# Group A's keys transposed in pairs of heads, and the second layer's units in another order

## The chip, the cores and the metric

The kernel runs on one core of a Trainium2 chip. The metric is the device time of one execution in microseconds. Three runs of the kernel before took 485.81, 486.31 and 487.1 us; the median is 486.31.

## The reference

Two layers, each with a residual connection around one mixer. A layer normalises its 512 x 1024 input, multiplies it by one combined matrix of 3488 columns, cuts the result into parts for four head groups A to D, multiplies each group's output by a SiLU gate, and sends all 1024 columns through an output matrix. The change touches group A, attention over four heads with low-rank queries and keys:

```python
    q = (rmsnorm(cq, mla_q_norm_g) @ mla_w_uq).reshape(B, S, MLA_HEADS, MLA_QK)
    kv = (rmsnorm(ckv, mla_kv_norm_g) @ mla_w_ukv).reshape(B, S, MLA_HEADS, MLA_NOPE + MLA_V)
...
    k = jnp.concatenate([k_nope, jnp.broadcast_to(k_rope, (B, S, MLA_HEADS, MLA_ROPE))], axis=-1)
    o_a = causal_attention_blocks(q, k, v_a, MLA_QK ** -0.5).reshape(B, S, GROUP_WIDTH)
```

A key has 96 numbers: 64 of its own head (`k_nope`, normalised) and 32 rotary ones (`k_rope`), which all four heads share. Queries have 96 too. All is in float32.

## The kernel before

**Tiling.** Tokens lie in four tiles of 128 (NT = 4). Every float32 product is made of three TensorE products of a high and a low part (`mm3`, line 283): an operand is split into `hi`, a copy rounded to the matmul's format, and `lo`, what is left of it, by one operation of ScalarE or VectorE and one of VectorE (`split2`, `split_scaled`).

**Order.** The program is unrolled Python. A small planner (`Order`, `Chain`, `Slots`, lines 75 to 214) runs generators against a clock of its own, prices each operation by a formula (lines 181 to 200; line 188 for VectorE, `cost` at line 217 for a matmul), and issues it on its engine when its inputs are due by that clock. So it fixes each engine's order of instructions; the hardware runs each engine's queue in that order and waits on semaphores. Main work (`main`) issues the large products, one unit of 24 matmuls after another; the heads' work is put between them when it is due, with a higher priority. A `Slots` object counts the buffers of a kind: a generator that asks for a buffer when none is free stops until one is put back, and other generators go on. The tag `t2` has NT2 = 11 buffers of 128 x 512 and serves nearly all temporaries: operands of the heads, gates, sums.

**Units.** In the second layer the order of units is SEQ1 (line 48). The names ga, gb, gc, gd are the gates of the four groups, su, ch, cc, cb inputs of groups B and C, each in two halves of 128 columns; p11, p21, p3, p4, p2, p1, p22 are the seven products from which the token-wise parts (sq: group C's second input and group D's queries; kv: group D's keys and values) are made. Then come seven more products of the output matrix (ZPROD, line 50): b11, t3, b21, t4, t2, t1, b22. b11 takes y tiles 2, 0, 1, 3 in this order (K0 and KK in line 49); y tiles 0 and 1 come from group A, 2 and 3 from group B (gated by gb0 and gb1), 4 and 5 from C, 6 and 7 from D. The first layer has another order (SEQ, line 382).

**Weights.** Units are loaded by SP's queue into `raw` buffers (`load_units`, line 407), split into `whi` and `wlo` by ScalarE and VectorE (`split_units`, `low_half`), and freed. Some weights are sums of others that DMAs add up in DRAM (`t_sums`, line 358, on SP's and POOL's queues).

**Group A.** `low_stats` (line 967) makes the rotary part of the keys, `krt`, 128 x 4 tiles x 32, turns it by six operations of VectorE (`rope`, line 916), and copies it with one POOL operation into columns 64 to 96 of all four heads of `L.K` (line 993); then event `kr_ev` is set. `q_chain` and `kv_chain` fill `L.Q` and the first 64 columns of `L.K`. `mla_heads` (line 1511) waits for all of these, in the second layer also for p4 (`mla_go`). For each head `prep` starts two generators `part` (line 1522): four transposes of 128 tokens x 96 into a PSUM bank (`t0` for queries, `t1` for keys), then the split into two `t2` buffers; keys are scaled by a column of gains, `pcol[0:96, 6 + l]`. When both are there, `qk` issues the scores (tile `sa`), four blocks with three matmuls each; `free` puts four `t2` buffers back, and the next head's `prep` begins.

**Mixer of group C.** `mix_chain` (line 1123) loads `sgw` when event `sg_go` comes (after the unit SGLOAD), masks it on POOL after `mix_go` (after p2), splits it, waits for the four normalised token tiles `vn`, lets MIXLAG pass on the planner's clock, and issues the products `mp`.

**Gains.** `load_rows` (line 615) loads rows of gains with DMAs from POOL's queue into a tile of ones; one transpose turns them into `pcol`.

Of the kernel before, what the change touches and what calls it, by code (L numbers as in the profile page):

```python
# [11 lines left out]
F32 = mybir.dt.float32  # L12
# [20 lines left out]
WSLACK = 300.0  # L33
AHEAD, URGENT, VSLACK = 4, 2, 300.0
NWARM, FILL, FILLEND = 6, 0.9, 15000.0
MIXT, MIXLAG, ROWT, COLT = 44000.0, 2000.0, 36000.0, 17500.0
KSPLIT, HMEAN = 6, 0.0
PAIRS = {}
LOPRIO = -5
# [5 lines left out]
STOK = (1,)  # L45
SPROD = ("p11", "p21", "p3", "p4", "p2", "p1", "p22")
SSUMS = {"p3": 0, "p2": 1, "p1": 2, "p22": 0}
SEQ1 = ['p11', 'ga0', 'p21', 'p3', 'p4', 'ga1', 'p2', 'ch0', 'p1', 'p22', 'cc0', 'gd0', 'gd1', 'su0', 'cb0', 'gb0', 'ch1', 'gc0', 'cc1', 'cb1', 'gb1', 'su1', 'gc1']
K0, K1, KK = (2, 3, 0, 1), (4, 5, 6, 7), (0, 2, 3, 1)
ZPROD = ("b11", "t3", "b21", "t4", "t2", "t1", "b22")  # L50
TS0 = 62000.0
SGLOAD = 'p4'
TAIL = ((0, 256), (256, 512))

C_CQ, C_KV, C_GA, C_CH, C_CB, C_CC, C_GB = 0, 256, 416, 672, 928, 1184, 1440
# [166 lines left out]
def hybrid_trunk(ctx: ExitStack, tc: tile.TileContext, x, positions, norm_g, w_c, w_f, w_t, w_o, mla_q_norm_g,  # L222
# [117 lines left out]

    tsum = {(l, n): dr.tile([2, P, 1024], F32, name=f"{n}_{l}") for l in SEVEN for n in ("t1", "t2", "t3", "t4")}
    tsum_ev = {(l, n, j): Event() for l, n in tsum for j in range(2)}
    ysc = {l: dr.tile([KT, P, S], F32, name=f"ysc_{l}") for l in SEVEN}

    def quad(l, n, j):
# [269 lines left out]
    def load_rows():  # L615
        pr = prow[0]
        nc.gpsimd.dma_start(pr[0:4, 0:P], dram(mla_q_norm_g, 0, [[P, 4], [1, P]]))
        nc.gpsimd.dma_start(pr[4:6, 0:P], dram(mla_kv_norm_g, 0, [[P, 2], [1, P]]))
        nc.gpsimd.dma_start(pr[6:8, 0:64], dram(mla_q_g, 0, [[96, 2], [1, 64]]))
        nc.gpsimd.dma_start(pr[10:12, 0:64], dram(mla_k_nope_g, 0, [[64, 2], [1, 64]]))  # L620
        for i, g in ((8, moba_q_g), (12, moba_k_g)):
            nc.gpsimd.dma_start(pr[i:i + 2, 0:P].rearrange("r (h d) -> r h d", h=2)[:, :, 16:64],
                              dram(g, 16, [[64, 2], [0, 2], [1, 48]]))
# [343 lines left out]
    def low_stats(L, t, a, t0, done):  # L967

        ch = Chain(o, t0)
        ssq, krt = L.ssq, L.krt  # L970
        for i, (c0, c1) in enumerate(((384, 416), (256, 384), (0, 256))):
            yield from ch.act(A.activation, junk[:, :c1 - c0], a[:, c0:c1], AF.Square, scale=(c1 - c0) ** -0.5,
                              accum_out=ssq[:, t, 2 - i:3 - i])
        m = sm.tile([P, 8], F32, tag="ms", name=f"ms{t}_{L.l}")
        e1, e2 = EPS, EPS * EPS
        if L.l == 0:
            yield from ch.wait(v_ev)
            e1, e2 = rv(RE, t), rv(REE, t)
        yield from ch.dve(V.tensor_scalar, m[:, 0:2], ssq[:, t, 1:3], 1.0, e1, op0=ALU.mult, op1=ALU.add)
        yield from ch.dve(V.tensor_scalar, L.e2[:, t, :], ssq[:, t, 0:2], EPS, e2, op0=ALU.mult, op1=ALU.add)  # L980
        yield from pow_rstd(ch, m[:, 4:6], m[:, 0:2], 2)
        L.ms[t] = m
        o.set(L.stat[t], ch.t)
        yield from ch.dve(V.scalar_tensor_tensor, krt[:, t, :], in0=a[:, 384:416], scalar=m[:, 5:6], in1=L.gr,
                          op0=ALU.mult, op1=ALU.mult)
        done(ch)
        L.kr_left -= 1
        if L.kr_left:
            return
        yield from ch.wait(rope_ev)  # L990
        yield from rope(ch, krt, 16, cosT, sinT, f"k{L.l}")
        yield from ch.wait(L.QK_ev)
        yield from ch.pool(G.tensor_copy, L.K[:, :, :, 64:96], krt.unsqueeze(2).to_broadcast([P, NT, 4, 32]))
        o.set(L.kr_ev, ch.t)

    def low_chain(L, t, a, t0, slots):
# [35 lines left out]
    def q_chain(L, t, q_ps, t0):  # L1032
        ch = Chain(o, t0)
        l = L.l
        if not L.QK_taken:
            L.QK_taken = True
            L.Q = yield from tkS.get(ch, f"Q{l}", 96)
            L.K = yield from tkS.get(ch, f"K{l}", 96)
            o.set(L.QK_ev, ch.t)
        yield from ch.wait(L.QK_ev)  # L1040
        Q = L.Q
# [469 lines left out]
    def mla_heads(L):  # L1511
# [3 lines left out]
        if L.stok:  # L1515
            yield from ch0.wait(L.mla_go)

        def prep(H):
            H.prep_ev = [Event(), Event()]
            H.op = [None, None]  # L1520

            def part(i, src):
                ch = Chain(o)
                tp = yield from trS.get(ch, f"t{i}{H.name}")
                for t in range(NT):
                    yield from ch.pe(109.0, PE.transpose, tp[:96, t * P:(t + 1) * P], src[:, t, H.h, :], ident)
                if H.h == 3:
                    tkS.put(ch)
                hi = yield from t2S.get(ch, f"hi{i}{H.name}", F32R)
                lo = yield from t2S.get(ch, f"lo{i}{H.name}", F32R)  # L1530
                if i == 0:
                    yield from split2(ch, hi[:96], lo[:96], tp[:96])
                else:
                    yield from split_scaled(ch, hi[:96], lo[:96], tp[:96], pcol[0:96, 6 + L.l:7 + L.l])
                trS.put(ch)
                H.op[i] = (hi, lo)
                o.set(H.prep_ev[i], ch.t)

            def free(ch):
                for _ in range(4):  # L1540
                    t2S.put(ch)
            H.free = free
            o.spawn(part(0, L.Q))
            o.spawn(part(1, L.K))
            return
            yield

        def qk(ch, H, qt, s):
            (qh, ql), (kh, kl) = H.op
            n = (qt + 1) * P  # L1550
            yield from mm3(ch, n, s, qh[:96, qt * P:n], ql[:96, qt * P:n], kh[:96, :n], kl[:96, :n], True, True)

# [573 lines left out]
```

## Time and profile before

| | |
|---|---|
| runs | 485.81, 486.31, 487.1 us; median 486.31 |
| span of the profiled execution, first to last instruction | 485.2 us |
| instructions of TensorE: matmuls, weight loads | 2432, 2432 |
| VectorE, ScalarE, POOL instructions | 898, 906, 189 |
| DMA packets, bytes | 40223, 92.89 MB, mean 191 GB/s |

The profile gives the span of its execution, and no separate time for it; the runs' median lies 1.1 us above the span.

The page of the profile gives each engine's busy time, then the span in 40 slices, then the chain of work that ended last, then groups of like instructions. A matmul's duration is a latency: the next one starts before it ends, so the time that an instruction takes from TensorE is the distance between starts, read in the order of time. In the tile view, the three numbers are the shortest, the median and the longest duration in ns, then come the first and the last start in us. A row of the waits reads: who waited, for whom, microseconds in total, times, the longest. In the view by stretches each engine's busy time is followed by its count of instructions, and the last three columns are the granted clock, the DMA engines' busy share and GB/s.

### The profile page before, as it was taken

How to read it: one execution, taken by the hardware profiler on the slowest of the kernel's cores; microseconds unless marked ns; L12 is line 12 of the kernel's file. 1: busy time of each engine (PE TensorE's matmuls, PEld its weight loads, DVE VectorE, ACT ScalarE, POOL GpSimd, SP SyncE). 2: the span in 40 equal slices, each digit the busy share in tenths (PEclk: the TensorE clock that was granted, in tenths of full speed). 3: DMA queues.
4: the chain of work that ended last, by engine and by line, in shares of the span. 5: the costliest groups of instructions: out<-in, count | busy, mean ns of one | idle time of the engine just before them, and what ended most of it. 6: DMA issues, size and time to landing. Idle time of an engine off the chain costs nothing.

```text
span 485.2 us, 7553 instructions
## 1 busy us (share of the span) xinstructions
PE 479.2 (99%) x2432; PEld 408.3 (84%) x2432; DVE 402.4 (83%) x898; ACT 330.7 (68%) x906; POOL 118.2 (24%) x189
## 2 busy tenths in 40 slices
PE   8999999999999999999999999999999999999996
PEld 7988888888888888888899888888888888888875
DVE  3598887877988898679998688797897889997992
ACT  6897857776466765457577799678766788576550
POOL 8857711610330014100031014630021300000000
PEclk9999999999999999999999999999999999999999
DMA  7923053998798499885673286696832826436862
GB/s 257 313 85 111 1 217 130 235 264 175 263 227 206 172 240 264 302 281 177 211 241 131 87 273 210 178 279 168 207 97 89 192 93 193 152 109 235 296 206 89
DMA packets 40223, 92.89 MB, mean 191 GB/s; under 512 B 5606, under 2 KB 21304, under 8 KB 39800
## 3 DMA queue, kind: packets, MB, share of 16 engines
q1 hardware_dynamic: 26864, 79.43, 46.9%
q0 software_dynamic: 13216, 12.91, 17.4%
q8 instruction: 19, 0.31, 0.3%
q14 instruction: 20, 0.16, 0.1%
q10 hardware_dynamic: 104, 0.07, 0.1%
HBM read 84.53 MB, written 33.03 MB: 242 GB/s over the span
## 4 chain that ended last, share of the span: by engine, by line
PE 90%; DVE 4%; DMA 3%; SPq 1%; issue 1%; ACT 0%; DVEq 0%
PE cq L209 6%; PE kv L209 6%; PE oy L209 5%; PE cb L209 5%; PE gb L209 5%; PE gc L209 5%; PE cc L209 5%; PE gd L209 5%; PE su L209 5%; PE ch L209 5%; PE ga L209 5%; PE sq L209 5%; PE py L209 3%; PE sa L209 3%; PE pz L209 2%; PE px L209 2%
## 5 line engine op out<-in xcount | busy, mean ns | idle before, releaser
L374 POOL DMA_DIRECT2D t<-in_w_o_dram x16 | 17.9, 1298 | 43.6 <-DMA t<-t 43.2
L179 ACT ACTIVATE pa<-pa,mna 128x384 f32<-128x384 f32 (+3 forms) x50 | 26.4, 554 | 2.1 <-DVE mna L179 2.1
L179 ACT ACTIVATE phd<-pTd 128x512 fp32r<-128x512 f32 (+3 forms) x32 | 13.9, 436 | 18.0 <-PE pTd L209 17.9
L179 DVE CUSTOM_DVE_ANT_0 pa<-sa,maskb,rs_q 128x512 f32<-128x512 f32 (+3 forms) x32 | 16.6, 548 | 10.2 <-PE sa L209 5.2
L179 ACT ACTIVATE whi_t<-raw_t 128x512 fp32r<-128x512 f32 x32 | 18.9, 620 | 5.5 <-DMA raw_t<-t 5.4
L179 ACT ACTIVATE pd<-pd,mnd 128x384 f32<-128x384 f32 (+3 forms) x38 | 20.7, 554 | 2.6 <-DVE mnd L179 2.1
L179 ACT ACTIVATE pha<-pTa 128x512 fp32r<-128x512 f32 (+3 forms) x32 | 13.9, 434 | 12.1 <-PE pTa L209 11.6
L209 PE MATMUL cq<-whi_c,hTh 128*128 128x416 f32 x64 | 20.7, 368 | 0.7 <-ACT hTh L179 0.7
L179 DVE TENSOR_TENSOR wlo_t<-raw_t,whi_t 128x512 fp32r<-128x512 f32 x32 | 20.6, 682 | 0.0
L209 PE MATMUL cq<-wlo_c,hTh 128*128 128x416 f32 x64 | 20.0, 358 | 0.0
L179 DVE TENSOR_TENSOR wlo_p<-raw_p,whi_p 128x512 fp32r<-128x512 f32 x28 | 19.0, 698 | 1.1 <-ACT whi_p L179 0.9
L209 PE MATMUL cq<-whi_c,hTl 128*128 128x416 f32 x64 | 19.8, 356 | 0.0
L179 ACT ACTIVATE whi_b<-raw_b 128x512 fp32r<-128x512 f32 x24 | 14.4, 623 | 7.6 <-DMA raw_b<-in_w_o_dram 7.6
L179 DVE TENSOR_TENSOR pla<-pTa,pha 128x512 fp32r<-128x512 f32 (+3 forms) x32 | 15.1, 486 | 5.1 <-ACT pha L179 5.0
L179 DVE CUSTOM_DVE_ANT_0 pd<-sd,maskb,rs_mq 128x512 f32<-128x512 f32 (+3 forms) x32 | 17.0, 545 | 2.6 <-PE pTd L209 2.3
L374 POOL DMA_DIRECT2D p<-in_w_t_dram x8 | 10.9, 1645 | 29.5 <-DMA p<-p 19.6
L179 DVE TENSOR_TENSOR pld<-pTd,phd 128x512 fp32r<-128x512 f32 (+3 forms) x32 | 15.5, 485 | 2.8 <-ACT phd L179 2.6
L179 DVE TENSOR_TENSOR wlo_b<-raw_b,whi_b 128x512 fp32r<-128x512 f32 x24 | 15.7, 683 | 0.1
L179 ACT ACTIVATE whi_p<-raw_p 128x512 fp32r<-128x512 f32 x25 | 15.0, 624 | 1.0 <-DMA raw_p<-in_w_t_dram 0.6
L179 POOL TENSOR_TENSOR rs_mk<-rs_mk,nhalf 128x16 f32<-128x16 f32 x2 | 6.1, 3074 | 33.8 <-DVE rs_mk L179 33.8
L209 PE MATMUL pTa<-ident,pa 128*128 128x128 f32 x80 | 14.1, 273 | 0.0
L179 POOL TENSOR_SCALAR xss<-xss 128x1 f32<-128x1 f32 x4 | 2.7, 669 | 46.6 <-ACT jk L179 42.3
(488 smaller groups left out, 1868.7 us busy)
## 6 DMA issues: line engine op xcount, KB each, us to landing
t<-in_w_o_dram POOLq DMA_DIRECT2D x16, 512.0 KB, 7.6
raw_t<-t SPq DMA_DIRECT2D x16, 512.0 KB, 5.0
raw_b<-in_w_o_dram SPq DMA_DIRECT2D x12, 512.0 KB, 4.4
t<-in_w_o_dram SPq DMA_DIRECT2D x8, 512.0 KB, 5.4
p<-in_w_t_dram POOLq DMA_DIRECT2D x8, 512.0 KB, 13.7
t<-t SPq DMA_DIRECT2D x8, 512.0 KB, 5.4
raw_p<-p SPq DMA_DIRECT2D x8, 512.0 KB, 4.4
ys<-ysc SPq DMA_DIRECT2D x14, 256.0 KB, 5.7
```

The source lines that it names most:

```text
L179: f(*a, **k)
L209: f(*a, **k)
L374: nc.gpsimd.dma_start(src(l, n, j), src(l, y, j), accum_op=ALU.add, max_dma_last_dim=1024)
```

## The change

The nope parts of the keys of two heads, 2 x 64 columns, are transposed together: four transposes of 128 x 128 a pair, whose upper 64 rows are one head and whose lower 64 rows the other. Each head's half is split into rows 0 to 64 of two `t2` buffers. The rotary part is transposed once a layer, all four tiles in one instruction of 128 x 128 (`krT`), scaled and split by one ScalarE and one VectorE operation, stored to DRAM (`krd`) by eight DMAs of SP, and loaded into rows 64 to 96 of each head's two key buffers by two DMAs of SP a head. A pair takes its four key buffers at its first head. `kr_ev` is set 3 us later on the planner's clock than the stores are issued. `L.K` gets 64 columns a head and no POOL copy. The gains' rows for `pcol` hold each gain twice, for both halves. In the second layer ga1, gd1, gc0, gb0 and others change places, `sgw` is loaded after p2 instead of p4, and MIXLAG is 1000 instead of 2000.

```diff
-MIXT, MIXLAG, ROWT, COLT = 44000.0, 2000.0, 36000.0, 17500.0
+MIXT, MIXLAG, ROWT, COLT = 44000.0, 1000.0, 36000.0, 17500.0
...
-SEQ1 = ['p11', 'ga0', 'p21', 'p3', 'p4', 'ga1', 'p2', 'ch0', 'p1', 'p22', 'cc0', 'gd0', 'gd1', 'su0', 'cb0', 'gb0', 'ch1', 'gc0', 'cc1', 'cb1', 'gb1', 'su1', 'gc1']
+SEQ1 = ['p11', 'ga0', 'p21', 'p3', 'p4', 'p2', 'ch0', 'p1', 'p22', 'cc0', 'gd0', 'ga1', 'su0', 'gc0', 'ch1', 'cc1', 'gd1', 'cb0', 'cb1', 'gb1', 'su1', 'gb0', 'gc1']
...
-SGLOAD = 'p4'
+SGLOAD = 'p2'
...
+    krd = {l: dr.tile([2, 32, S], F32, name=f"krd_{l}") for l in range(DEPTH)}
...
-        nc.gpsimd.dma_start(pr[6:8, 0:64], dram(mla_q_g, 0, [[96, 2], [1, 64]]))
-        nc.gpsimd.dma_start(pr[10:12, 0:64], dram(mla_k_nope_g, 0, [[64, 2], [1, 64]]))
+        for i, g, w in ((6, mla_q_g, 96), (10, mla_k_nope_g, 64)):
+            nc.gpsimd.dma_start(pr[i:i + 2, 0:P].rearrange("r (h d) -> r h d", h=2), dram(g, 0, [[w, 2], [0, 2], [1, 64]]))
...
-        yield from ch.wait(L.QK_ev)
-        yield from ch.pool(G.tensor_copy, L.K[:, :, :, 64:96], krt.unsqueeze(2).to_broadcast([P, NT, 4, 32]))
+        tp = yield from trS.get(ch, f"krT{L.l}")
+        yield from ch.pe(109.0, PE.transpose, tp[:, 0:P], krt.rearrange("p t d -> p (t d)"), ident)
+        z = yield from t2S.get(ch, f"kr{L.l}", F32R)
+        f = -(96 ** -0.5)
+        yield from ch.act(A.activation, z[:, 0:P], tp[:, 0:P], AF.Copy, scale=f)
+        yield from ch.dve(V.scalar_tensor_tensor, z[:, P:2 * P], in0=tp[:, 0:P], scalar=f, in1=z[:, 0:P].bitcast(F32),
+                          op0=ALU.mult, op1=ALU.subtract)
+        trS.put(ch)
+        for i in range(2):
+            for t in range(NT):
+                nc.sync.dma_start(krd[L.l][i, :, t * P:(t + 1) * P], z[t * 32:(t + 1) * 32, i * P:(i + 1) * P].bitcast(F32))
+        ch.t += 3000.0
+        t2S.put(ch)
         o.set(L.kr_ev, ch.t)
...
-            L.K = yield from tkS.get(ch, f"K{l}", 96)
+            L.K = (yield from tkS.get(ch, f"K{l}", 96)).rearrange("p a b c -> p (a b c)")[:, 0:D]
+            L.K = L.K.rearrange("p (t h d) -> p t h d", t=NT, h=4)
...
+            def keys():
+                ch = Chain(o)
+                c2, w = Chain(o), {}
+                for y in range(2):
+                    for i in range(2):
+                        w[y, i] = yield from t2S.get(c2, f"k{i}{y}{H.name}", F32R)
+                        dma(c2, P * 512, w[y, i][64:96, :].bitcast(F32), krd[L.l][i])
+                    o.set(pair["dma", y], c2.t)
+                tp = yield from trS.get(ch, f"t1{H.name}")
+                for t in range(NT):
+                    yield from ch.pe(109.0, PE.transpose, tp[:, t * P:(t + 1) * P],
+                                     L.K[:, t, 2 * hp:2 * hp + 2, :].rearrange("p h d -> p (h d)"), ident)
+                if hp == 1:
+                    tkS.put(ch)
+                for y in range(2):
+                    a0 = y * 64
+                    yield from split_scaled(ch, w[y, 0][0:64], w[y, 1][0:64], tp[a0:a0 + 64],
+                                            pcol[a0:a0 + 64, 6 + L.l:7 + L.l])
+                    pair[y] = w[y, 0], w[y, 1]
+                    o.set(pair["ev", y], max(ch.t, pair["dma", y].t))
+                trS.put(ch)
...
-            o.spawn(part(0, L.Q))
-            o.spawn(part(1, L.K))
+            if x == 0:
+                for y in range(2):
+                    pair["ev", y], pair["dma", y] = Event(), Event()
+                o.spawn(keys())
+            o.spawn(queries())
+            H.prep_ev[1] = pair["ev", x]
...
-            (qh, ql), (kh, kl) = H.op
+            (qh, ql), (kh, kl) = H.op[0], pair[H.h % 2]
```

`queries` is the old `part` for the queries alone.

More of the change, by code (lines that the diff above doesn't have):

```diff
@@ L1516, in mla_heads @@
             yield from ch0.wait(L.mla_go)
+        pair = {}
         def prep(H):
@@ L1520, in prep, with queries @@
             H.op = [None, None]
-            def part(i, src):
+            hp, x = H.h // 2, H.h % 2
+            def queries():
                 ch = Chain(o)
-                tp = yield from trS.get(ch, f"t{i}{H.name}")
+                tp = yield from trS.get(ch, f"t0{H.name}")
                 for t in range(NT):
-                    yield from ch.pe(109.0, PE.transpose, tp[:96, t * P:(t + 1) * P], src[:, t, H.h, :], ident)
+                    yield from ch.pe(109.0, PE.transpose, tp[:96, t * P:(t + 1) * P], L.Q[:, t, H.h, :], ident)
@@ L1527, in part @@
                 if H.h == 3:
                     tkS.put(ch)
[L1529 to L1534, printed above, removed]
-                trS.put(ch)
-                H.op[i] = (hi, lo)
-                o.set(H.prep_ev[i], ch.t)
+                hi = yield from t2S.get(ch, f"hi0{H.name}", F32R)
@@ new lines, in queries @@
+                lo = yield from t2S.get(ch, f"lo0{H.name}", F32R)
+                yield from split2(ch, hi[:96], lo[:96], tp[:96])
+                trS.put(ch)
+                H.op[0] = (hi, lo)
+                o.set(H.prep_ev[0], ch.t)
+            def keys():
[19 more added lines that the diff above has]
+                trS.put(ch)
```

## The prediction

> **What bounds the kernel now.** I read the page first, then TensorE's own list of waits, then its order of time.
>
> ```profile
> span 485.2 us, 7553 instructions
> PE 479.2 (99%) x2432; PEld 408.3 (84%) x2432; DVE 402.4 (83%) x898; ACT 330.7 (68%) x906; POOL 118.2 (24%) x189
> ...
> PE   8999999999999999999999999999999999999996
> ...
> PE 90%; DVE 4%; DMA 3%; SPq 1%; issue 1%; ACT 0%; DVEq 0%
> ```
>
> ```profile
> PE cq L209 <- ACT hTh L179: 0.7, 3, 0.3
> PE oy L209 <- DVE xr L179: 0.2, 1, 0.2
> ```
>
> ```profile
> 230.60 13.61 PE oy L209 x60
> ```
>
> TensorE is busy in every slice (its granted clock is 1.00 in every stretch shown below), and is 90% of the chain that ended last. A busy share alone can hide gaps, since matmuls overlap; so I look at the pace. In the chain, 60 matmuls of 512 columns take 13.61 us, 0.227 us from start to start, without a gap. Apart from the warm-up, TensorE's list has 0.9 us of waits: at a layer's first products (cq) and once in a last phase (oy), none in the middle of a layer. So an instruction that leaves TensorE takes its pace off the end time, and nothing else can take off much. An instruction of TensorE that has to wait adds its wait in full, because the queue is in order and the main products stand behind it.
>
> **The change part by part.**
>
> Transposes. Before, each of 4 heads transposes its keys with 4 instructions (line 1526 on src = L.K): 16 a layer. After, each pair of heads does so with 4 instructions of 128 rows by 128 columns: 8 a layer, and one more (tile krT) turns the rotary part of all 4 token tiles at once. 16 - 8 - 1 = 7 a layer, 14 in both.
>
> ```profile
> 340.03 0.39 PE L209 MATMUL cc<-hTh,wlo_cc 128*128 128x512 f32 x1
> 340.27 0.60 PE L209 MATMUL t1a<-ident,K 128*96 128x128 f32 x4
> 340.62 0.48 PE L209 MATMUL cc<-hTh,whi_cc 128*128 128x512 f32 x1
> ...
> 341.17 0.40 PE L209 MATMUL cc<-hTh,wlo_cc 128*128 128x512 f32 x1
> ```
>
> ```profile
> 380.17 0.39 PE L209 MATMUL gb<-hTh,wlo_gb 128*128 128x512 f32 x1
> 380.40 0.60 PE L209 MATMUL tmqd<-ident,mq 128*128 128x128 f32 x4
> 380.84 0.60 PE L209 MATMUL tmkd<-ident,mk 128*128 128x128 f32 x4
> 381.19 0.47 PE L209 MATMUL gb<-hTh,whi_gb 128*128 128x512 f32 x1
> 381.51 0.39 PE L209 MATMUL gb<-hTl,whi_gb 128*128 128x512 f32 x1
> ```
>
> Durations overlap, so the price is the pace. From 340.03 to 341.17 there are three matmuls of 0.227 (the third left out here) and 4 transposes: (1.14 - 0.68) / 4 = 0.115 us each. From 380.17 to 381.51 there are two matmuls and 8 transposes of full 128 columns, the shape that the keys get: (1.34 - 0.45) / 8 = 0.111 us. I take 0.111: 14 x 0.111 = **1.55 us** off. Bounds: 14 x 0.115 = 1.61, and 14 x 0.109 = 1.53 (back-to-back starts 0.44 / 4 = 0.11, less rounding).
>
> The same rows test a rule of the Trainium skill that speaks against wider transposes: "TensorE: Matmul & The Clock Gate", section "LDWEIGHTS (loading the stationary operand)", has the load's time grow with the columns loaded, 80 ns for 96 and 107 ns for 128 by its formula.
>
> ```profile
> L209 PEld LDWEIGHTS t1a<-ident,K x32: 123/126/132, 65.9 to 367.2; 128*96 128x96 f32 x32
> L209 PEld LDWEIGHTS tmkd<-ident,mk x16: 139/140/142, 134.5 to 405.6; 128*128 128x128 f32 x16
> ```
>
> The trace has 126 and 140 ns: longer, by a ninth, and yet four transposes start 0.35 us before the next instruction in both shapes (340.27 to 340.62, 380.84 to 381.19). By that row the wider load costs no pace. What it would give if it did is a rival below.
>
> The split of the keys, and small things. The gains' rows take as many DMAs as before, with each row twice. Four ScalarE or VectorE operations of 96 x 512 and four of VectorE a layer become as many of 64 x 512. Group D's key splits have the new shape already:
>
> ```profile
> L179 DVE SCALAR_TENSOR_TENSOR lo1a<-t1a,pcol,hi1a x8: 733/737/747, 67.7 to 369.8; 96x512 fp32r<-96x512 f32 x8
> L179 DVE SCALAR_TENSOR_TENSOR kl0d<-tmkd,pcol,mk0d x4: 711/740/745, 136.7 to 407.5; 64x512 fp32r<-64x512 f32 x4
> ```
>
> 737 and 740 ns: nothing gained or lost. New a layer: one ScalarE copy and one VectorE operation of 128 x 128, some 0.4 us together by the rotary steps below (0.22 us for 64 columns), beside engines at 68% and 83%; gone is one POOL copy. None is waited for by TensorE in the list above; I put them at 0. If that cover were gone they would cost 0.4 us a layer at most.
>
> krT on TensorE. This is the added wait: before, only the POOL copy read the rotated krt; now an in-order TensorE instruction does, with the sq products of the first layer, or ga0 and p11 of the second, behind it.
>
> ```profile
> 49.69 1.63 DVE L179 TENSOR_TENSOR rbk<-krt,sinT 128x64 f32<-128x64 f32 x2
> ...
> 52.03 0.35 DVE L179 TENSOR_TENSOR krt<-krt,rbk 128x64 f32<-128x64 f32 x2
> ```
>
> ```profile
> 281.15 0.23 DVE L179 TENSOR_TENSOR rbk<-krt,sinT 128x64 f32<-128x64 f32 x1
> ...
> 285.98 0.22 DVE L179 TENSOR_TENSOR krt<-krt,rbk 128x64 f32<-128x64 f32 x1
> ```
>
> The order of instructions is fixed by the kernel's planner, which prices a rotary step at 68 + 1.047 x 64 = 135 ns (line 188). In the first layer the six steps ran from 49.69 to 52.38, 2.69 us for a planned 0.81; in the second from 281.15 to 286.20, 5.05 us for a planned 4.1 (six steps, four weight splits of 0.604 between them, a reduction of 0.47 and a split of 0.40 by the same formula). If all of that lateness fell on TensorE it would be 1.9 + 0.95 = 2.8 us; the lower end is 0, since TensorE is behind its plan too (0.227 against a planned 0.215 a matmul). TensorE takes up many results of ScalarE and VectorE planned in this way (cT, pTa, tmqd) and its list shows 0.1 to 0.3 us only at "cq"; nearest to that row, I take 0.1 a layer, **0.2 us** lost.
>
> The way over DRAM. Eight stores of 16 KB a layer and four loads of 64 KB a pair, all issued by SP, with weight loads behind them and the splits and products behind those.
>
> ```profile
> L1198 SPq DMA_DIRECT2D ysc<-chs x1: 320/320/320, 432.3 to 432.3; - x1
> ```
>
> ```profile
> SPq L296 <- DVE wlo_cb L179: 36.5, 4, 10.0
> ```
>
> At 0.32 us an issue, the eight stores hold SP for 2.6 us once a layer and the four loads for 1.3 us a pair. SP is covered: its weight loads wait for a raw buffer to be split free (36.5 us in four waits for cb's alone), so a later issue is a shorter wait; without that cover a product could be 2.6 us late. krt is ready at 52.4 and the first heads start at 65.6, so the loads find the stores landed. But the pair's first scores now wait for the loads too.
>
> ```profile
> 65.59 0.60 PE L209 MATMUL t0a<-ident,Q 128*96 128x128 f32 x4
> ...
> 69.94 0.40 PE L209 MATMUL sa<-hi1a,hi0a 96*128 96x512 f32 x1
> ```
>
> ```profile
> out_dram<-xr SPq DMA_DIRECT2D x1, 64.0 KB, 2.1
> gq_b<-in_mla_q_g_dram SPq DMA_DIRECT2D x1, 16.0 KB, 6.6
> ```
>
> ```profile
> 66.00:70.00 4.00, 4.00 (x25) 3.48 (x24) 3.26 (x6) 2.76 (x6) 0.00 (x0) 1.00 0.33 103
> 84.00:90.00 6.00, 6.00 (x35) 5.22 (x35) 5.92 (x17) 5.85 (x20) 6.00 (x7) 1.00 1.04 323
> 318.00:334.00 16.00, 16.00 (x79) 13.22 (x78) 14.79 (x30) 14.37 (x54) 3.93 (x5) 1.00 1.02 241
> 350.00:362.00 12.00, 12.00 (x70) 10.36 (x69) 10.79 (x30) 8.33 (x20) 0.72 (x1) 1.00 0.37 81
> ```
>
> From a head's first transpose to its first scores the trace leaves 4.35 us. A small transfer lands in 2.1 us (64 KB, quiet) to 6.6 us (16 KB, busy start). The last two columns of the stretches are DMA share and GB/s: two of the four pairs fall into quiet ones (0.33, 0.37), two into full ones (1.04, 1.02). I take the quiet row, and 0: the planner sets the scores after the load it prices. The upper end is 6.6 - 4.35 = 2.25 us in each of the two full stretches, 4.5 us.
>
> Buffers. A pair holds six of the eleven t2 buffers (four of keys, two of queries) where a head held four. A head that gets no buffer waits outside the queue and main products go on, so the price is 0 while there are main products left.
>
> The second layer's order. Each unit keeps its 24 matmuls, so no work leaves; it can only move waits. ga1 goes from before p2 to after gd0 (one gate less held during the first heads); sgw is loaded after p2 instead of p4, and the mixing products may follow 1 us sooner (MIXLAG); the mixer still waits for the normalised tokens that p2 itself produces, so the mask that POOL lays over sgw, with POOL's weight sums queued behind it, has that long; price 0. gb0 becomes the last but one, and the first product after the units (b11) starts with its result, y tile 2.
>
> ```profile
> L209 PE MATMUL gb<-hTh,wlo_gb x8: 389/390/397, 420.0 to 426.5; 128*128 128x512 f32 x8
> L179 ACT ACTIVATE yTh<-chs x1: 620/620/620, 433.3 to 433.3; 128x512 fp32r<-128x512 f32 x1
> ```
>
> gb's last matmul ends at 426.9 and its y tile is there at 434.0, 7.1 us later; the cover is gc1's 24 x 0.227 = 5.4 us and the heads' work between. From 0 to 1.7 us lost; I take 0, as this VectorE queue is emptier at the very end. What could be won is one hole in the last phase: 469.47 to 470.06, 0.59 us for a matmul of 0.227, **0.4 us**.
>
> ```profile
> 469.47 0.39 PE L209 MATMUL oy<-whi_t,suml 128*128 128x512 f32 x1
> ...
> 470.06 0.47 PE L209 MATMUL oy<-whi_t,sumh 128*128 128x512 f32 x1 [0.20 <-DVE xr L179]
> ```
>
> The sum: -1.55 + 0.2 = -1.35 us; the span goes from 485.2 to 483.85. The runs' median 486.31 lies 1.1 us above this span, for what lies around it; so 486.31 - 1.35 = **485.0 us**.
>
> **The rivals.**
>
> More comes off: krT never waits and the hole of 0.4 us closes because heads end earlier: -1.55 - 0.4 = -1.95, 484.4 us. For it: heads 2 and 3 of group A start without ga1's gate held. Against: that hole waits for VectorE, whose work stays.
>
> Given back: krT waits for the late rotary steps, or b11 for y tile 2. Half of 2.8 us is 1.4: -1.55 + 1.4, 486.2 us; the full bounds give 487.6. For it: 2.69 us where 0.81 were planned. Against: no such wait in TensorE's list.
>
> The weight load sets the pace: nine transposes at 140/126 of the price, 16 x 0.111 - 9 x 0.123 = 0.67 a layer, 1.33 in both; less 0.2, 485.2 us. Against: 0.35 us in both shapes. By the figures of that section of the Trainium skill, 107/80, it would be 485.6 us.
>
> Slower: the rotary rows land late. Place: the first scores of the two pairs in full stretches. Price: 2 x 2.25 us, -1.35 + 4.5 = +3.15, 489.5 us. It decides from a landing of 5.8 us on, where 2 x 1.45 outweighs the gain by as much as can be told. For it: DMA shares of 1.04 and 1.02. Against: in the first of those stretches the trace leaves 6.7 us, not 4.35:
>
> ```profile
> 86.65 0.61 PE L209 MATMUL t0a<-ident,Q 128*96 128x128 f32 x4
> ...
> 93.37 0.48 PE L209 MATMUL sa<-hi1a,hi0a 96*128 96x512 f32 x1
> ```
>
> **How the numbers follow.** About 0.3% (1.46 us, below 484.85) is what a measurement of this kernel can tell from no change, and my forecast lies beside that line. Forecast 0.50, half of it beyond the line; more off 0.20, faster; given back 0.15, nearly all within; weight load 0.03, within; slower 0.12, of which 0.02 would stay within. That makes faster 0.45, same 0.43, slower 0.12. The range runs from the first rival's 484.4 less 0.4 of run-to-run spread, 484.0, to 487.0, most of the way to the full give-back; outside are most of the slower rival and a little below.
>
> **What would show it.** TensorE with 2418 instructions and some 1.5 us less busy time; t1a as 16 instructions of 128 columns with the pace of tmkd; two krT. In TensorE's list of waits a row "krT <- DVE krt" over 0.5 us speaks for the give-back, a row "sa <- DMA" for the slow rival. I am wrong if the count falls and the span doesn't without such a row, or if waits appear where units were reordered.

## The result, and the profile after

| | before | after |
|---|---|---|
| median of 5 runs | 486.31 us | 491.00 us (490.25 to 493.55) |
| ratio, 95% interval | | 1.0093 [1.0066, 1.0119] |
| span of the profiled execution | 485.2 us | 490.1 us (its run: 491.83 us) |
| TensorE instructions | 2432 | 2418 |

The change is slower, by 4.5 us (3.2 to 5.8); forecast were 485.0 us, 484.0 to 487.0. The page of the changed kernel, first lines, slices of TensorE and of its clock:

```profile
span 490.1 us, 7563 instructions
...
PE 480.8 (98%) x2418; PEld 408.5 (83%) x2418; DVE 402.0 (82%) x892; ACT 332.2 (68%) x892; POOL 113.6 (23%) x187
...
PE   8999999999999999999999999978999999999996
...
PEclk9999999999999999999999999989999999999999
```

The 14 instructions are gone. TensorE, busy in nine tenths of every slice but the first and the last before, has a 7 and an 8 in the slices from 318 to 343 us, and the clock has an 8 in the first of them. TensorE's list of waits names the places:

```profile
PE py L209 <- DVE x L179: 2.5, 1, 2.5
PE gd L209 <- DVE Mt L179: 1.5, 1, 1.5
```

Before, no wait stood in the middle of a layer. Both new ones do: the second layer, where its units were reordered. The first in TensorE's order of time, and then the same stretch by windows (the last three columns are granted clock, DMA share, GB/s):

```profile
320.36 0.39 PE L209 MATMUL py<-whi_p,yTl 128*128 128x512 f32 x1
323.25 0.47 PE L209 MATMUL py<-whi_p,yTh 128*128 128x512 f32 x1 [2.50 <-DVE x L179]
```

```profile
320.00:323.25 3.25, 0.75 (x5) 0.32 (x3) 2.65 (x5) 3.25 (x7) 3.17 (x3) 1.00 0.01 3
323.25:327.00 3.75, 3.75 (x10) 2.95 (x11) 3.64 (x8) 3.75 (x14) 2.94 (x3) 0.56 0.35 43
```

From start to start it is 2.89 us where the pace is 0.227: 2.66 lost. Then the granted clock is 0.56 for 3.75 us, which loses 3.75 x 0.44 = 1.65 more. With the second stop, 1.66 by the same measure (337.98 to 339.86), these are 6.0 us. The hole of 0.4 us in the last phase is closed, but one of the same size is new in the first layer (oy, 231.14 to 231.75), so less the 1.55 us of the transposes 4.4 of the 4.9 us between the spans are named; the other 0.5 us isn't traced to single rows.

What TensorE waited for is told by VectorE's order of time and by the tile sgw, the mixer's weights, after the change:

```profile
320.61 0.69 DVE L179 TENSOR_TENSOR wsl<-sgw,wsh 128x512 fp32r<-128x512 f32 x1 [4.26 <-ACT wsh L179]
321.21 1.29 DVE L179 TENSOR_TENSOR yTl<-a,yTh 128x512 fp32r<-128x512 f32 x2
322.42 0.68 DVE L179 TENSOR_TENSOR x<-py,x 128x512 f32<-128x512 f32 x1
```

```profile
L296 SPq DMA_DIRECT2D sgw<-in_sg_w_dram x2: 422/423/424, 43.0 to 309.8; - x2
L179 POOL TENSOR_SCALAR_AFFINE_SELECT sgw<-sgw x2: 645/646/647, 50.4 to 319.3; 128x512 f32<-128x512 f32 x2
...
  DMA sgw<-in_sg_w_dram: 5.4, 1
  ACT wsh L179: 4.3, 1
  POOL sgw L179: 4.1, 1
```

and the same tile before:

```profile
L296 SPq DMA_DIRECT2D sgw<-in_sg_w_dram x2: 333/378/422, 42.9 to 305.3; - x2
L179 POOL TENSOR_SCALAR_AFFINE_SELECT sgw<-sgw x2: 647/1046/1445, 50.6 to 312.3; 128x512 f32<-128x512 f32 x2
```

The last start of each row is the second layer's. The load is issued 4.5 us later than before, the mask starts 7.0 us later, at 319.3, 9.5 us after the issue. POOL waits 5.4 us for the DMA, ScalarE's split of sgw 4.1 us for POOL, VectorE's other half 4.3 us for ScalarE. Behind that half stand the sum `x<-py,x`, which frees a PSUM bank, and TensorE's next product into that bank. A chain over four in-order queues, begun by one load of 256 KB. Why that load took 9.5 us is the subject of the last experiments.

The second wait, gd for Mt, ends a chain of the same kind. VectorE's order of time:

```profile
334.33 0.43 DVE L179 CAST whi_ga<-raw_ga 128x512 fp32r<-128x512 f32 x1 [3.15 <-DMA raw_ga<-in_w_f_dram]
336.76 0.43 DVE L179 CAST whi_su<-raw_su 128x512 fp32r<-128x512 f32 x1 [2.01 <-DMA raw_su<-in_w_f_dram]
338.97 0.41 DVE L179 TENSOR_TENSOR Mt<-x,Mt 128x256 fp32r<-128x256 f32 x1
```

The loads of ga1 and su0 were issued at 327.1 and 328.6 and landed after 7.2 and 8.1 us; POOL had issued a pair of its weight sums at 324.1. VectorE waits for both loads, and Mt, which TensorE waits for, stands behind them.

### The profile page after: what moved, and what is told of

It reads as the page before. It is cut to its first block, busy times and chain, and to the rows that moved or that the text cites. A ratio compares the mean times of both kernels' runs of the same rounds, so it can differ in the third digit from the quotient of the medians.

```text
span 490.1 us, 7563 instructions
## 1 busy us (share of the span) xinstructions
PE 480.8 (98%) x2418; PEld 408.5 (83%) x2418; DVE 402.0 (82%) x892; ACT 332.2 (68%) x892; POOL 113.6 (23%) x187
## 5 line engine op out<-in xcount | busy, mean ns | idle before, releaser
L179 ACT ACTIVATE pa<-pa,mna 128x128 f32<-128x128 f32 (+3 forms) x55 | 28.3, 541 | 4.8 <-DVE mna L179 4.6
L179 ACT ACTIVATE pd<-pd,mnd 128x128 f32<-128x128 f32 (+3 forms) x46 | 24.1, 542 | 4.6 <-DVE mnd L179 4.4
L375 POOL DMA_DIRECT2D t<-in_w_o_dram x16 | 16.9, 1288 | 30.0 <-DMA t<-t 30.0
L179 POOL TENSOR_TENSOR rs_mq<-rs_mq,nhalf 128x16 f32<-128x16 f32 x2 | 6.4, 3178 | 43.3 <-DVE rs_mq L179 25.7
L209 PE MATMUL gd<-hTh,whi_gd 128*128 128x512 f32 x32 | 13.4, 419 | 1.5 <-DVE Mt L179 1.5
L375 POOL DMA_DIRECT2D p<-in_w_t_dram x8 | 9.8, 1486 | 21.2 <-DMA p<-in_w_t_dram 10.8
```

The costliest lines, as they stand in the source:

```text
L179: f(*a, **k)
L209: f(*a, **k)
L375: nc.gpsimd.dma_start(src(l, n, j), src(l, y, j), accum_op=ALU.add, max_dma_last_dim=1024)
```

## The experiments

The theories. **S**: the late sgw is the loss. **K**: a pair's six t2 buffers hold the heads back until the main products run out. **O** (later **G**, for ga1): the new order of units costs time by itself. **P** came last: POOL's weight sums, DMAs of 512 KB, hold up the loads beside them. Against these stands **D**: the way over DRAM or krT costs it. All ratios are to the kernel before, run beside.

**1. sgw earlier, all else as in the changed kernel.** SP issues the second layer's load after p4 again, into a buffer set aside for it (`sg_own`); no other engine's order is touched.

```diff
-        dma(ch, P * 2048, sgw, sg_w[l])
+        if l:
+            o.clk["D"] = max(o.clk["D"], ch.t) + P * 2048 / 360.0
+            ch.t = o.clk["D"] + 2000.0
+        else:
+            dma(ch, P * 2048, sgw, sg_w[l])
...
+                nc.sync.dma_start(sg_own[0].rearrange("p (g s) -> p g s", g=4), sg_w[l])
```

> The changed kernel with one DMA moved: the second layer's sgw load is issued at the end of p4 instead of p2, three places earlier in SP's queue; every engine's order of instructions stays as it was. Theory S (the late sgw load holds ScalarE and VectorE, and p22's products wait behind them): the wait 'py <- DVE x' of 2.5 us goes, the granted clock of 0.56 after it goes back to 1.00 (1.6 us), together 4.1 us less, 486.9 us; 485.3 if gd's wait of 1.5 us is a consequence too. Theory O (the new order of units leaves too little between p2 and p22, whenever sgw lands) and theory K (a pair of heads holds six buffers and comes late): still 490 to 491 us, with the wait of 2.5 us.

Measured: 487.51 us (485.6 to 489.78, 10 runs), 1.0017 [1.0000, 1.0035]. The mask now starts at 312.8 us, and the wait of py is gone from TensorE's list; pTa (1.8 us), gd (1.6) and t0a (1.0) are left. VectorE waits 4.4 us for ga1's load there, issued 4.0 us behind a pair of sums. So the place of one DMA in SP's queue is worth (1.0093 - 1.0017) x 486 = 3.7 us, most of the loss.

**2. sgw late in the kernel before.** The reverse: only that load goes three loads later, behind the wait for `mix_go`.

```diff
-            dma(ch, P * 2048, sgw, sg_w[l])
+            if l:
+                o.clk["D"] = max(o.clk["D"], ch.t) + P * 2048 / 360.0
+                ch.t = o.clk["D"] + 2000.0
+            else:
+                dma(ch, P * 2048, sgw, sg_w[l])
         if L.stok:
             yield from ch.wait(L.mix_go)
+            nc.sync.dma_start(sgw, sg_w[l])
```

> The kernel before, with one thing changed: the second layer's load of sgw stands three loads later in SP's queue, after p2's loads instead of p4's; every engine's own order stays. Theory S (the late mask weights are the loss): the load lands behind the three others, VectorE's split of sgw waits and TensorE's next unit waits for the tokens queued behind it on VectorE; 1 to 4 us slower, 488 to 490 us, with a wait of TensorE for VectorE near the first products of group C's chain. Theory O (the loss lies in the new order of units, and the late load is harmless in itself): 486.0 to 487.0 us, within 0.3% of before.

Measured: 495.8 us (494.78 to 496.56, 4 runs), 1.0184 [1.0169, 1.0198]: S, with over twice the loss expected. The load's landing and TensorE's wait:

```profile
DMA to landing us min/median/max: 9.3/9.3/9.3
```

```profile
322.87 0.38 PE L209 MATMUL t1a<-ident,K 128*96 128x128 f32 x2
329.33 0.66 PE L209 MATMUL t1a<-ident,K 128*96 128x128 f32 x2 [6.08 <-DVE K L179]
```

Issued at 316.9, landed at 326.2; in the old order the split of sgw stands ahead of the keys that the first transposes read, so TensorE stops in the middle of a group of four for 6.1 us.

**3. The two numbers of the planner.** The changed kernel with sgw after p4 in the plan too; then with MIXLAG put back to 2000 as well.

```diff
-SGLOAD = 'p2'
+SGLOAD = 'p4'
```

> The changed kernel with SGLOAD = 'p4' as before, so that the planner knows of the early load and shifts other instructions a little. Theory S: 485 to 487 us, without the wait of py. Theories O and K: 490 to 491 us.

> The changed kernel with both planner numbers put back (sgw after p4, the mixing products 2 us later), so that only the order of units and the pairs of keys differ from before. By the plan the last head of group D ends after 21.4 of the output's units where the run with sgw alone put back had 19.2 and the kernel before 20.2. Theory K (six buffers a pair hold the heads back, and the end of the main products leaves them uncovered): 489 to 498 us, with TensorE waiting for VectorE in the last 40 us. Theory O': the numbers of units don't matter, 487.0 to 488.5 us like the run with sgw alone put back.

Measured: 487.75 us (486.32 to 490.55, 10 runs), 1.0023 [1.0004, 1.0041], as in run 1; and 497.86 us (497.53 to 498.04, 4 runs), 1.0226 [1.0213, 1.0240]. In the first one sgw is issued at 300.2 and masked at 307.1. POOL waits 5.2 us of these 6.9 for the load, but no other engine waits for it: it is ahead of its use. In the second, 1 us of lag on the planner's clock decides some 10 us. Apart from gd's 1.6 us its longest waits lie at the end (ox for `yad` 2.2, oz 2.3 in three), as K expects of heads that finish late.

**4. The keys alone: pairs, krT and DRAM in the old order of units** (SEQ1, SGLOAD and MIXLAG as before), and the kernel before with six buffers a pair but its old keys and no DRAM (`reserve` takes a buffer and leaves it unused):

```diff
+                if i == 1 and H.h % 2 == 0:
+                    for _ in range(2):
+                        yield from t2S.reserve(ch)
...
+            if H.h % 2 == 1:
+                for _ in range(2):
+                    t2S.put(Chain(o))
```

> The keys' part alone: pairs of heads, krT and the way over DRAM, with the order of units, SGLOAD and MIXLAG of before. Theories S and O: the 14 transposes less show, -1.55 us and up to 0.5 us of new waits: 484.7 to 485.3 us. Theory K: slower than before, 487 us or more, with waits of TensorE at the heads' first scores or at units that wait for buffers.

> The kernel before, with its 16 transposes of keys a layer and no way over DRAM; only each pair's first head of group A takes two more t2 buffers (unused, handed back before the second head's begins), so that a pair holds six as in the changed kernel. The plan delays the second layer's heads as in the run of the pairs alone in the old order (first scores after 8.5 units of the output, last head of D after 21.5; before 7.1 and 20.2). Theory K (buffers): 494 to 500 us, with waits of pTd, ox or the like for VectorE at 440 to 470 us. Theory D (the stored and reloaded rotary rows or krT cost the time in that run): 486 to 487 us.

Measured: 498.33 us (497.65 to 498.64, 4 runs), 1.0236 [1.0220, 1.0251], and 496.88 us (496.1 to 497.89, 4 runs), 1.0208 [1.0195, 1.0221]. The waits of the first and of the second:

```profile
PE pTd L209 <- DVE pld L179: 4.5, 2, 3.9
PE ox L209 <- DVE yad L179: 1.8, 1, 1.8
```

```profile
PE pTd L220 <- DVE pld L190: 3.7, 2, 2.1
PE ox L220 <- DVE yad L190: 1.8, 1, 1.8
```

The same two, without a single paired transpose in the second kernel: two buffers held and not even used cost 10 us. pTd and ox belong to group D's last heads and the product behind them, at 450 to 460 us.

**5. One buffer more.** The keys' tile takes a third less in the changed kernel; with a place of its own, what is left over is a twelfth t2 buffer. In the old order of units, then in the new one (with sgw after p4):

```diff
-NRAW, NW, NT2 = 2, 6, 11
+NRAW, NW, NT2 = 2, 6, 12
...
-    tkS = Slots(o, 2, lambda name, d: tkp.tile([P, NT, 4, d], F32, tag="tk", name=name))
+    tkS = Slots(o, 1, lambda name: tkp.tile([P, NT, 4, 96], F32, tag="tk", bufs=1, name=name))
+    kkS = Slots(o, 1, lambda name: tkp.tile([P, NT, 4, 64], F32, tag="kk", bufs=1, name=name))
...
```

> The run of the pairs alone in the old order of units, with a twelfth t2 buffer (the keys' tile is a third smaller in the changed kernel, and takes a place of its own of that size; what is left over is one buffer more). By the plan the last head of group D ends after 20.6 of the output's units; 21.5 with eleven buffers, 20.2 in the kernel before. Theory K (buffers held by a pair delay the heads past the end of the main products): most of the loss of 11.6 us goes, 486 to 490 us, with less than 2 us of TensorE waiting after 440 us. Rival (something else in the pairs, the reloaded rows or krT, costs the time): 496 us or more, as with eleven.

> The changed kernel with sgw loaded after p4 again and a twelfth t2 buffer in the same way. With eleven buffers it took 487.75 us and its profile showed the heads' start late (1.6 us of stalls at 330 to 340 us). Theory K: these go, and the transposes' 1.55 us show: 485.0 to 486.5 us. Rival (what is left there is VectorE's and ScalarE's work before the heads, not buffers): 487 to 489 us, with TensorE still waiting at 328 to 340 us.

Measured: 488.33 us (487.19 to 489.25, 10 runs), 1.0033 [1.0019, 1.0046], and 490.99 us (489.77 to 491.67, 6 runs), 1.0080 [1.0062, 1.0099]. By windows, the stretch where the heads end, with eleven buffers and with twelve:

```profile
450.00:465.00 15.00, 8.73 (x27) 6.47 (x26) 12.30 (x25) 7.90 (x17) 0.00 (x0) 0.66 0.62 211
```

```profile
450.00:465.00 15.00, 14.50 (x64) 11.68 (x63) 14.07 (x28) 7.50 (x16) 0.00 (x0) 1.00 0.87 302
```

27 matmuls against 64 in the same 15 us: in the old order one buffer takes back 10 of the 11.6 us, which is K from the other side. In the new order it gains nothing; the run is slower than that with eleven, and above both ranges. TensorE waits elsewhere there:

```profile
335.14 0.61 PE L209 MATMUL t0a<-ident,Q 128*96 128x128 f32 x4 [1.74 <-DVE Q L179]
```

Ahead of it ScalarE waits 3.2 us for gd0's load and VectorE 2.8 us for ScalarE (more of this below). So whether the twelfth buffer would help in the new order without that late load isn't shown.

**6. The order alone, with the old keys**: first with sgw after p2 and lag 1000 as in the change, then SEQ1 alone.

> The second layer alone: order of units, SGLOAD = 'p2' and MIXLAG = 1000 of the change, keys as before (16 transposes a layer). Theories S and O: 4 to 6 us slower than before, 490 to 492 us, with a wait of py for VectorE in the p22 products and a clock below 1.00 behind it. Theory K: 486 to 487 us, no such wait.

> The kernel before with the second layer's new order of units alone: old keys, sgw after p4, lag 2 us. With sgw after p2 and lag 1 us the new order took 492.3 us. Theory O1 (the order itself crowds ScalarE and VectorE before the heads, since p2 and the tokens after it come one unit earlier): 490 to 493 us. Theory O2 (sgw's place and the shorter lag made that loss): 486.5 to 488 us.

Measured: 492.28 us (490.95 to 493.42, 4 runs), 1.0117 [1.0091, 1.0143], and 489.71 us (489.42 to 492.5, 5 runs), 1.0071 [1.0044, 1.0098]. The order costs 3.4 us by itself (2.1 to 4.8); its time lies just under O1's range. In the first run of the two the wait of py that S and O expected doesn't come: sgw is masked 4.0 us after its issue and only 0.4 us are waited for it. That loss is not S. What both share is ScalarE's wait for gd0's weights, here of SEQ1 alone, then TensorE's wait:

```profile
325.30 0.63 ACT L179 ACTIVATE whi_gd<-raw_gd 128x512 fp32r<-128x512 f32 x1 [3.25 <-DMA raw_gd<-in_w_f_dram]
```

```profile
329.52 0.64 PE L209 MATMUL t0a<-ident,Q 128*96 128x128 f32 x4 [0.98 <-ACT mix L179]
```

raw_gd is issued at 318.44 and taken up at 325.30; the mixer's results stand behind it on ScalarE, and the first head's transposes wait for them.

**7. ga1 back before p2**, with the old keys (after the run of SEQ1 alone), and with the new keys and twelve buffers (after the slower run of 5):

```diff
-SEQ1 = ['p11', 'ga0', 'p21', 'p3', 'p4', 'p2', 'ch0', 'p1', 'p22', 'cc0', 'gd0', 'ga1', 'su0', 'gc0', 'ch1', 'cc1', 'gd1', 'cb0', 'cb1', 'gb1', 'su1', 'gb0', 'gc1']
+SEQ1 = ['p11', 'ga0', 'p21', 'p3', 'p4', 'ga1', 'p2', 'ch0', 'p1', 'p22', 'cc0', 'gd0', 'su0', 'gc0', 'ch1', 'cc1', 'gd1', 'cb0', 'cb1', 'gb1', 'su1', 'gb0', 'gc1']
```

> The run of the new order of units alone (old keys, sgw after p4, lag 2 us; 489.7 us), with ga1 back in its old place before p2. Theory G (ga1's place is the loss of the order: without that unit of 5.4 us the weights of gd0 and the tokens before the heads come late): 486.0 to 487.0 us, ScalarE's wait for raw_gd near 320 to 330 us down from 3.3 us to under 1.5, and no wait of t0a. Rival (gd1, gc0, gb0 or the rest of the order costs it): 489 to 491 us.

> The new keys with a twelfth t2 buffer, sgw after p4, lag 1 us, new order of units (490.99 us), with ga1 back before p2. Theories G and K together (ga1's place and the buffers were the losses): 485.0 to 487.0 us, no wait of t0a near 333 us, and near or under the kernel before. Rival: 489 us or more, with a wait of TensorE for VectorE or ScalarE at another place.

Measured: 493.52 us (492.95 to 495.34, 4 runs), 1.0145 [1.0125, 1.0166], a miss in the time, and 487.58 us (486.45 to 488.88, 12 runs), 1.0017 [1.0005, 1.0029], by the ratios 3.1 us faster than without, a little above the range. In both, ScalarE's wait for raw_gd is down to 0.4 and 0.8 us and no wait of t0a is left, as G said of the place. But in the first a wait appears at another place:

```profile
389.74 0.68 DVE L179 TENSOR_TENSOR yaa<-oa,oba 64x512 f32<-64x512 f32 x1 [4.88 <-DMA ysc<-yaa]
390.45 0.69 DVE L179 TENSOR_TENSOR mq1d<-tmqd,mq1d 64x512 fp32r<-64x512 f32 x1
```

```profile
391.30 0.88 PE L209 MATMUL pTa<-ident,pa 128*128 128x128 f32 x4 [4.16 <-DVE mq1d L179]
```

VectorE waits 4.9 us for the one `yaa` buffer to be stored, with group D's query split behind it, and TensorE waits behind that. So ga1's place makes the waits at 325 to 335 us; the total of an order can't be told from that place alone.

**8. The new keys in the first layer alone**, second layer as before:

```diff
+            (qh, ql), (kh, kl) = H.op if L.l else (H.op[0], pair[H.h % 2])
...
+        yield from heads(L, "a", L.Vt, prep1 if L.l else prep, qk)
...
```

> The pairs of heads, krT and the way over DRAM in the first layer alone; the second layer as before in keys, order of units, sgw and lag. Seven transposes fewer. Theory K and S: nothing is lost in the first layer, since main products cover the heads there: 7 x 0.111 = 0.8 us faster, 485.6 to 486.2 us against 486.5. Theory D (the way over DRAM or krT costs time): slower than before by 1 us or more, with a wait for the key rows or krT in the first layer.

Measured: 486.83 us (485.48 to 487.64, 12 runs), 0.9995 [0.9987, 1.0004]. No wait for krT or for the rows from DRAM is in TensorE's list, and D's loss of 1 us or more is excluded; but of the 0.8 us at most 0.6 came out, and the time lies above the range of K and S. The profile shows small stops that the kernel before doesn't have, such as one at the end of group D's heads, where od's products, at 187.89, 188.42 and 189.02 us, follow each other by 0.53 and 0.60 us.

**9. POOL's weight sums.** In the changed kernel POOL issues a pair of weight sums at 302.3 us; in the first run of 6 at 309.0. With the same loads ahead of sgw in SP's queue, this is what SP's loads issued from 300 to 313 us took to land, the last column, after the change and there:

```profile
t<-in_w_o_dram POOLq DMA_DIRECT2D x2, 512.0 KB, 13.2
raw_p<-in_w_t_dram SPq DMA_DIRECT2D x2, 512.0 KB, 8.7
raw_cc<-in_w_f_dram SPq DMA_DIRECT2D x1, 512.0 KB, 9.0
```

```profile
raw_p<-in_w_t_dram SPq DMA_DIRECT2D x2, 512.0 KB, 3.7
t<-in_w_o_dram POOLq DMA_DIRECT2D x2, 512.0 KB, 8.2
raw_cc<-in_w_f_dram SPq DMA_DIRECT2D x1, 512.0 KB, 3.6
```

So four kernels move a pair in POOL's queue and leave the order of every other engine as it was. In the changed kernel: behind the mask, and behind two more POOL operations.

```diff
-                nc.gpsimd.dma_start(src(l, n, j), src(l, y, j), accum_op=ALU.add, max_dma_last_dim=1024)
+                def add(l=l, n=n, y=y, j=j):
+                    nc.gpsimd.dma_start(src(l, n, j), src(l, y, j), accum_op=ALU.add, max_dma_last_dim=1024)
+                if (l, n) == (1, "t1"):
+                    held.append(add)
+                else:
+                    add()
...
+        if l == 1:
+            assert len(held) == 2
+            for add in held:
+                add()
...
```

> The changed kernel with every engine's order and SP's queue untouched; only POOL's pair of weight sums (two DMAs of 512 KB that add to DRAM, issued at 302.3 us before) is issued after the mask over sgw instead of before it. In the changed kernel SP's loads of 512 KB in that stretch landed after 6.4 to 9.0 us and sgw after 9.5; in the run of the order alone, where POOL's pair came at 309.0 us, SP's landed after 3.7 us and sgw within 4. Theory P (POOL's pair holds SP's loads up, so the load of sgw is late because of what is beside it, not only because of its place): sgw's mask at 314 to 316 us, the wait of py under 0.5 us, 486.5 to 489 us. Rival (three loads ahead in SP's own queue are enough): mask at 318 us or later, 490 to 492 us.

> The changed kernel with POOL's first pair of weight sums issued still later: behind the next two powers on POOL (near 321 us), so that it stands neither beside sgw's load (issued at 310) nor beside gd0's (issued at 317). With the pair moved behind the mask alone, sgw landed in time, but ScalarE then waited 3.8 us for raw_gd, and the time stayed (491.2 us). Theory P (POOL's pair delays whichever SP load is in flight beside it by 3 to 5 us, and this is what both the late sgw and the new order's late gd0 are): ScalarE's wait for raw_gd under 1 us, no wait of py, t0a and t1a over 0.5, 486.5 to 489 us. Rival (gd0's weights are late by the order in SP's queue): the wait for raw_gd over 2.5 us, 490 to 492 us.

Measured: 491.2 us (489.52 to 491.55, 4 runs), 1.0088 [1.0063, 1.0113], and 488.81 us (487.5 to 489.84, 10 runs), 1.0037 [1.0021, 1.0053]. In the first, sgw is masked at 314.3 us, 4.3 us after its issue, and the wait of py is 0.3 us: P's mechanism. The time stays all the same, for the pair, now issued at 314.9, stands beside gd0's load, issued at 317.3. That load's landing and what ScalarE makes of it, then the same with the pair still later, at 319.2:

```profile
raw_gd<-in_w_f_dram SPq DMA_DIRECT2D x1, 512.0 KB, 7.2
```

```profile
324.52 0.63 ACT L179 ACTIVATE whi_gd<-raw_gd 128x512 fp32r<-128x512 f32 x1 [3.83 <-DMA raw_gd<-in_w_f_dram]
```

```profile
raw_gd<-in_w_f_dram SPq DMA_DIRECT2D x1, 512.0 KB, 3.5
```

```profile
320.62 0.63 ACT L179 ACTIVATE whi_gd<-raw_gd 128x512 fp32r<-128x512 f32 x1 [0.18 <-DMA raw_gd<-in_w_f_dram]
```

One pair of sums, two loads that it can hit, and either hit costs some 2.5 to 4 us (run 1 and the two here). The wait of gd for Mt, 1.5 us, stays in both, and so does VectorE's wait for ga1's load beside the second pair, 4.1 and 4.2 us; t0a still waits 0.7 us in the later one. The same move of the second pair, for the order alone with the old keys (SEQ1 alone of 6) and for the changed kernel with sgw after p4 (first of 3):

```diff
+                if (l, n) == (1, "t3"):
+                    o.held = getattr(o, "held", ()) + (add,)
...
```

> The run of the new order alone with old keys (489.7 us; ScalarE waits 3.3 us for raw_gd), with POOL's second pair of weight sums (issued there at 317.2, raw_gd at 318.4) issued behind a later operation of POOL, at 354 us; nothing else differs. Theory P: raw_gd lands within 5 us, ScalarE waits under 1 us for it, t0a no longer waits, 486.5 to 488 us. Rival (the order leaves gd0's load too little time in any case): a wait over 2.5 us, 489 to 491 us.

> The changed kernel with sgw after p4 (487.75 us) and POOL's second pair of weight sums, issued there at 317.6 and 319.4 beside the loads of gd0, ga1, su0 and the key rows, issued behind a later operation of POOL. Theory P: the waits that were left before the first heads (mp 0.6, gd 0.4, t0a 0.3 us; ScalarE 1.3 us for raw_ga) go, 485.5 to 487 us, near or under the kernel before. Rival (those waits are ScalarE's and VectorE's own work): 487.3 to 488.5 us.

Measured: 488.01 us (486.42 to 489.48, 10 runs), 1.0022 [1.0007, 1.0038], where it was 1.0071; raw_gd lands after 3.5 us and isn't waited for. And 486.13 us (485.38 to 487.23, 12 runs), **0.9983 [0.9971, 0.9994]**: the new keys in the new order, with sgw early and the second pair of sums clear of the loads of gd0, ga1 and su0, are 0.8 us faster than the kernel before (0.3 to 1.4), the only version here that is. The first sums still stand beside sgw's load, and POOL waits 5.5 us for it, but nothing else does. Its list of waits, apart from the warm-up:

```profile
PE gd L213 <- DVE zz L179: 0.4, 1, 0.4
PE od L213 <- DVE pld L179: 0.2, 1, 0.2
```

## Why the prediction was wrong

Of the prediction's signs of being wrong the last one came: waits where units were reordered.

**The second layer's order: the step that failed.** The prediction put sgw's later load at 0, as "the mixer still waits for the normalised tokens that p2 itself produces, so the mask that POOL lays over sgw, with POOL's weight sums queued behind it, has that long". Two things are wrong in it. It looked at who needs sgw in the end (the products mp), not at what stands behind the splits of sgw on ScalarE and VectorE; in the profile of before, the mask came 7.0 us after the issue and didn't wait for the load, so it showed no such chain. And it named POOL's weight sums as something that waits behind the mask; in the changed kernel a pair is issued at 302.3, ahead of it, and is what makes the load late: 512 KB each in flight beside it. Experiments 1 and 2 and the first run of 9 show the step: 3.7 us gained and 8.9 lost by that load's place, and its mask brought from 9.5 us behind the issue to 4.3 by the sums' place.

**ga1's move** was counted as a gain ("one gate less held during the first heads"). It also brings gd0's load forward, from 323.9 us in the kernel before to 318.4 in the run of SEQ1 alone, 1.3 us behind a pair of sums issued at 317.2. The run of twelve buffers in the new order is such a hit too: a pair at 317.4, gd0's load at 318.7. Two edits end ScalarE's wait for it. Moving the sums lets it land after 3.5 us. Putting ga1 back doesn't keep the sums away: with the new keys the load, issued at 322.6, is taken up 6.6 us later, with POOL's queue busy beside it, and yet ScalarE waits only 0.8 us. So sgw and gd0 have this in common: a load beside POOL's sums, with its first reader near. Of the 3.4 us that the order costs alone, moving the sums took back 2.4; the other 1.0 isn't traced.

**Buffers.** That "the price is 0 while there are main products left" has a true condition that wasn't examined. In the old order with lag 2000 they were not left: six buffers a pair cost 10 us there (experiments 4 and 5). With the new order of units, sgw early and lag 1000 the same keys took 487.75 us, with the new order and lag 2000 497.86. So the new order by itself doesn't pay for the buffers; with the shorter lag it does. The old order with the shorter lag wasn't run, so what the lag does alone stays open.

**The clock.** The sum had no term for it. 1.65 of the 6.0 us of the two stops are TensorE at about half speed after the first.

**What held.** TensorE's count is 2418. (Its busy time didn't fall by 1.5 us as foreseen but rose from 479.2 to 480.8; the stretch at half speed is 1.65 us of that, the rest isn't traced.) The pace of a group of four at 128 columns is unchanged, 333.87 to 334.22:

```profile
333.87 0.60 PE L209 MATMUL t1a<-ident,K 128*128 128x128 f32 x4
334.22 0.48 PE L209 MATMUL cc<-hTh,whi_cc 128*128 128x512 f32 x1
```

so the 14 transposes left TensorE's work, and the rival of the weight load falls. No row krT stands in the list of waits: 0, not 0.2. b11 doesn't wait for y tile 2, and the hole of 0.4 us in the last phase is gone. With the second pair of sums clear of the loads, 0.8 of the 1.55 us show in the median (last run of 9). The rest, and the 0.8 us of run 8, aren't settled: small stops such as od's may take them back, which no run here shows.

**The rival "rotary rows land late"** was right about the landing and wrong about its price. In the changed kernel, DMAs issued from 328 to 331.5 us:

```profile
k00a<-krd SPq DMA_DIRECT2D x1, 64.0 KB, 8.1
```

```profile
342.00 0.40 PE L209 MATMUL sa<-k00a,hi0a 96*128 96x512 f32 x1
```

8.1 us is above the upper end of 6.6. But the load was issued at 328.98, and its first scores came 13 us later, so nothing waited for it; no row "sa <- DMA" stands in TensorE's list of any run. The change was slower, but not by this path.

**The chances** were added up wrongly: with 0.02 of the slower rival counted as within, same is 0.45 and slower 0.10, not 0.43 and 0.12.

## What to carry to other kernels

When a load or the work around it is moved, look for the load's first reader on each in-order engine, for what stands behind that reader, and for the large transfers of other queues that will now be in flight beside it. Where a planner writes out the order, a resource held longer (here two buffers) or a unit moved is no local edit: run each part alone, and expect that a part can cost more than the whole (here 11.6 us for the new keys in the old order, 4.5 us for all).

## What the runs showed of the hardware

**Stops of TensorE can halve its clock.** The granted clock after stops of TensorE, by windows: here two stretches of the changed kernel after its wait of 2.5 us, one of run 7's first kernel after 4.2 us, one of run 1's after 1.8 us:

```profile
325.00:327.00 2.00, 2.00 (x6) 1.52 (x6) 2.00 (x5) 2.00 (x9) 1.19 (x2) 0.50 0.61 73
327.00:329.00 2.00, 2.00 (x10) 1.65 (x9) 2.00 (x6) 1.59 (x10) 0.00 (x0) 0.97 1.10 162
```

```profile
391.00:394.50 3.50, 3.21 (x10) 2.69 (x11) 3.47 (x8) 1.96 (x3) 0.00 (x0) 0.58 0.19 26
```

```profile
395.00:400.00 5.00, 4.89 (x24) 4.03 (x25) 4.82 (x15) 3.78 (x12) 0.00 (x0) 1.00 0.02 3
```

After 1.8 us it stayed at 1.00, after 2.5 us it fell to 0.50 and was back some 4 us later. So a stop of 2.5 us cost 4.3. The length of one stop doesn't decide alone: in the second run of 3 two stops of TensorE, of 1.0 us until 443.45 and of 0.5 until 444.70, were followed by a granted clock of 0.50 from 446 to 448 us. The Trainium skill ("TensorE: Matmul & The Clock Gate", section "Part 1: The HAM clock gate (the "warmup" mystery)") has half the clock after an idle window of about 3.4 us, which runs freely, and the full clock after a busy one. The half and the time to come back agree with the rows; the length of the stop does not: a wait of 2.5 us was enough here.

**One queue's sums hold up another queue's loads.** In the rows of experiment 9 a load of 512 KB on SP's queue landed after 3.5 to 3.7 us without, and after 7.2 to 9.0 us beside, a pair of POOL's accumulating DMAs; 64 KB of key rows took 8.1 us beside them. It is no fixed factor: in the kernel before, gd0's load, issued 0.5 us behind a sum, landed after 4.8 us. Nor do the times of issue tell a hit by themselves: in the first run of 6 raw_cc was issued 0.1 us behind the pair and landed after 3.6 us; POOL's queue moved 0.05 MB there from 300 to 313 us, and 0.91 MB in the changed kernel. The Trainium skill ("DMA: Bandwidth & Descriptors", section "Issuing engines are not separate DMA queues") says that DMAs of all issuing engines run on the same 16 DMA engines and interleave: the rows agree, and give the price.
